# Sublayer outputs of a two-layer hybrid decoder: three projections from channels on the partitions to tokens on the partitions

## The chip, the cores and the metric

The kernel runs on one core of one Trainium2 chip. A core has TensorE (PE, matrix products into PSUM banks), VectorE (DVE), ScalarE (ACT), GpSimd (POOL) and SyncE (SP, which here issues DMAs). The metric is the device time of one execution, in microseconds; the median of several runs is compared.

## The reference

Batch 1, 512 tokens, model width 1024, two layers, all in float32. Layer 0 mixes tokens with an RG-LRU block, layer 1 with gated linear attention (GLA); each mixer is followed by a gated ConvFFN with 2816 hidden channels.

```python
c_act = silu(c)
for i in range(2):
    sh_m, sc_m, gt_m, sh_f, sc_f, gt_f = split(c_act @ ada_w[i] + ada_b[i], 6)
    h = rmsnorm(x, norm_g[i, 0]) * (1 + sc_m) + sh_m
    y = rglru_mixer(h) if i == 0 else gla_mixer(h)      # both end with  ... @ w_out  (1024 x 1024)
    x = x + gt_m * rmsnorm(y, norm_g[i, 1])
    h = rmsnorm(x, norm_g[i, 2]) * (1 + sc_f) + sh_f
    u = causal_dwconv3(h @ w_up); g, val = split(u, 2)
    y = (gelu(g) * val) @ w_down                        # 2816 x 1024
    x = x + gt_f * rmsnorm(y, norm_g[i, 3])
```

So there are four sublayers, each of which ends with a projection to y, a norm over the 1024 channels of y, a gated addition to the residual x and, but for the last, a norm over x and a scale and shift that make the next h. The change concerns the ends of the first three; the last one is already in the form that they get.

## The kernel before, in words

**Products.** Every float32 product is done as three matmuls on values that are split into a rounded high part and a low part: high x high, high x low, low x high (`mm3`, and the same three lines in `strassen` and `down_t`). A weight unit is 128 x 1024 floats (512 KB). SP loads it into a slot of the ring `raw` (3 slots), ScalarE casts the high part into a slot of the ring `w` (8 slots), and VectorE subtracts to get the low part. For the units that `BYLOAD` names, ScalarE writes the negated high part instead and a DMA from POOL's queue adds the unit from memory onto it. General tiles of 128 x 512 come from the ring `g` (43 slots), half ones from `gh`, products land in seven PSUM banks `mm`, small sums in an eighth, `nr`.

**A planner orders the work.** The program adds operations with a cost each to a list; `Sched.order` plays them on modelled engines and fixes the order of every engine's instructions and the slots. TensorE and SP take the ready operation that was added first; the others take the one with the longest modelled path behind it. On the chip each engine runs its instructions in that fixed order and waits on semaphores.

**Channels on the partitions.** x, h and the mixers' values lie with 128 channels on the partitions and tokens along the row. x fills `xbuf` in that form from the start. In `out_proj`, which ends the RG block, the first feed-forward layer and GLA, the weights are the stationary operand and the activations move. `FULL` (1, 2, 2) output tiles are computed over all 512 tokens; the others first over tokens 0 to 255, then 256 to 511, so that the first half's normalisation runs while TensorE works on the second half. A norm over channels is then a sum over partitions: ScalarE squares, VectorE adds the eight tiles, TensorE multiplies with a column of ones (`rstd_bcast`), POOL takes the power -0.5, TensorE broadcasts it. This is done once for y and once for the new x in each half: four times in each `out_proj`, twelve in all. The next projection begins in halves as well: `proj_halves` computes the first `NAH` = 7 units over one half of the tokens, then over the other.

**The feed-forward layers.** 22 pairs of hidden tiles (`up`) alternate with parts of the down projection. In layer 0 the hidden tiles are summed in `DOWN_GROUPS`: tiles 0-3 and 8-9 directly, 4-7 and 10-13 by Strassen's seven products (`strassen_cols`, moving width 256), 14-21 in `out_proj`. In layer 1 tiles 0-17 go through Strassen with the activations stationary and the weights moving, width 512 (`strassen`, groups of `SGROUPS`), and y has tokens on the partitions; tiles 18-21 follow directly in `down_t`. There x is turned by VectorE in two steps of 16 transposes of 32 x 32 blocks (`turn_x`), and `gate_rows` makes the gate as two rows over channels.

**adaLN.** The modulation columns are 1024-long products of c with rows of `ada_w`, 96 units of 512 KB, each one VectorE operation (`ada`). Sixteen are made at the start; 80 wait in `ada_queue` and are taken by `ada_some`: 24 (`ADA_A`) ahead of the RG output, 4 (`ADA_B`) behind it, 4 per pair (`ADA_F`) in layer 0's feed-forward until none is left. Their ring `araw` has two slots; the GLA's attention rows (`both` in `inter_mm`) and layer 1's hidden quarters use the same ring.

Of the kernel before, what the change touches and what calls it, by code (L numbers as in the profile page):

```python
# [8 lines left out]
F32 = mybir.dt.float32  # L9
# [18 lines left out]
DOWN_GROUPS = ((0, 4), (4, 8), (8, 10), (10, 14), (14, 22))  # L28

SGROUPS = ((0, 4), (4, 8), (8, 12), (12, 16), (16, 18))
SLAST = (18, 22)
SPARTS = (3,), (4, 2), (5, 6), (7, 1)
SFIRST = (1, 3)
# [11 lines left out]
def sunits(gi):  # L48

    a, b = SGROUPS[gi]  # L50
    if b - a == 4:
        return [((i, 0), (i, 1)) for part in SORDER for i in part]
    return [((3, 0), (4, 0)), ((2, 0), (5, 0)), ((6, 0), (7, 0)), ((1, 0),)]


def sfind(gi, i, j):

    for u in sunits(gi):
        if (i, j) in u:
            return ("st", gi, u), u.index((i, j))  # L60


def last_ffn():

    steps, done = [], 0
    for gi, (a, b) in enumerate(SGROUPS):
        for part in SORDER:
            while done < min(b + 1, KF):
                steps.append(("up", done))
                done += 1  # L70
            steps += [("st", gi, i) for i in part]
            b += 1
# [11 lines left out]
def unit_list():  # L84
# [12 lines left out]
    for m in range(KD):  # L97
        u.append((("rgo", m), "rg_w_out", [(k, m) for k in range(KD)]))
# [4 lines left out]

    def ffn(layer):
        if layer == 1:
            for what, *i in last_ffn():
                if what == "up":
                    pair(1, *i)
                    continue
                gi, n = i  # L110
                key, c = sfind(gi, n, 0)
                if c == 0:
                    a = SGROUPS[gi][0]
                    u.append((key, "dn1", [(a + 2 * j + SPROD[n_][0][0], 4 * SPROD[n_][0][1] + m)
                                           for n_, j in key[2] for m in range(4)]))
            for k in range(*SLAST):
                u.append((("dnt", k), "dn1", [(k, m) for m in range(KD)]))
            return
        done = 0
        for gi, (a, b) in enumerate(DOWN_GROUPS):  # L120
            if gi in SFIRST:
                while done < b + 1:
                    pair(layer, done)
                    done += 1
                for part in SPARTS:
                    for n in part:
# [1558 lines left out]
```

## Time and profile before

| | |
|---|---|
| runs, median (lowest to highest), 3 runs | 1146.86 us (1146.44 to 1147.57) |
| span of the profiled execution, first to last instruction | 1145.5 us |
| TensorE busy | 1130.3 us, 6219 instructions |
| VectorE busy | 973.1 us, 1734 instructions |
| ScalarE busy | 627.0 us, 993 instructions |
| GpSimd busy | 92.3 us, 115 instructions |
| read from memory | 203.0 MB, 179 GB/s over the span |

For the profiled execution nothing but its span is given; the runs' median lies 1.4 us above it. The stages in TensorE's timeline: the RG block's input projection from about 18 us, its output projection from about 132 to 182, the first feed-forward layer to about 542 (its `out_proj` from 508), GLA to about 800 (its output projection from about 745), then the second feed-forward layer. Line 552 is the one line that issues every matmul, 475, 489 and 500 VectorE's two-input, three-input and one-input operations, 525 and 532 ScalarE's, 480 POOL's power, 980 the transposes of x. Matmuls are pipelined, so the durations of single ones overlap, and a stretch's length over its count is the better price of one.

### The profile page before, as it was taken

What the parts mean: (1) busy time and instruction counts of PE and PEld (TensorE: products, weight loads), DVE (VectorE), ACT (ScalarE), POOL (GpSimd) and SP (SyncE); (2) the same over time, 40 slices, a digit from 0 to 9 for tenths busy, and PEclk for the clock granted to TensorE, in tenths of its full rate; (3) what the DMA queues carried; (4) which work ended last, traced back from release to release, by engine and by line L of the source; (5) the groups of instructions that cost most, each with busy time, mean ns of one, the idle gap of its engine ahead of it and who ended that gap; (6) DMA issues with size and microseconds to landing.
All of it is one profiled execution on the core that took longest, in us unless ns stands there. A gap on an engine that the chain in (4) does not pass through costs nothing.

```text
span 1145.5 us, 16668 instructions
## 1 busy us (share of the span) xinstructions
PE 1130.3 (99%) x6219; PEld 977.9 (85%) x6219; DVE 973.1 (85%) x1734; ACT 627.0 (55%) x993; POOL 92.3 (8%) x115
## 2 busy tenths in 40 slices
PE   8999999999999999999999999999999999999997
PEld 6876899988888888889997888899988888888886
DVE  7998999966888898788959989549788898999998
ACT  5499864655435444543559645445656545363443
POOL 1000000001000010000100100100010100101001
PEclk9999999999999999999999999999999999999999
DMA  9868663588777987964571703323366677878631
GB/s 368 294 207 282 205 237 112 165 249 239 201 193 222 262 257 202 288 206 146 141 228 44 189 14 112 125 59 86 81 154 177 162 178 193 201 186 203 147 111 74
DMA packets 57651, 206.19 MB, mean 180 GB/s; under 512 B 6401, under 2 KB 6913, under 8 KB 57570
## 3 DMA queue, kind: packets, MB, share of 16 engines
q1 hardware_dynamic: 46914, 166.59, 42.6%
q0 software_dynamic: 10656, 38.54, 19.3%
q8 instruction: 49, 0.80, 0.3%
q14 instruction: 32, 0.26, 0.1%
HBM read 203.00 MB, written 2.10 MB: 179 GB/s over the span
## 4 chain that ended last, share of the span: by engine, by line
PE 85%; DVE 6%; ACT 4%; issue 2%; DMA 1%; POOL 1%; DVEq 0%; SPq 0%; POOLq 0%; ACTq 0%
PE mm L552 83%; PE nr L552 2%; ACT g L525 2%; DVE gh L475 1%; DVE g L475 1%; ACT L525 1%; DVE const L475 1%; DVE gh L489 1%; DVE w L475 1%; POOL sm L480 1%; DMA araw<-in_adaT_dram 0%; DVE const L489 0%; ACT w L532 0%; DMA raw<-in_wall_dram 0%; DMA const<-in_xT_dram 0%
## 5 line engine op out<-in xcount | busy, mean ns | idle before, releaser
L552 PE MATMUL mm<-g,w 128*128 128x512 f32 (+1 forms) x4342 | 822.4, 349 | 0.1
L552 PEld LDWEIGHTS mm<-g,w 128*128 128x128 f32 x4342 | 702.7, 189 | 104.9 <-issue 1.4
L532 ACT CAST w<-raw 128x1024 fp32r<-128x1024 f32 x198 | 203.7, 1039 | 117.1 <-DMA raw<-in_wall_dram 84.7
L475 DVE TENSOR_TENSOR w<-raw,w 128x1024 fp32r<-128x1024 f32 x157 | 189.3, 1212 | 24.6 <-ACT w L532 24.3
L489 DVE SCALAR_TENSOR_TENSOR g<-mm,const,g 128x510 f32<-128x510 f32 (+2 forms) x199 | 147.1, 747 | 58.6 <-ACT g L525 48.1
L525 ACT ACTIVATE g<-mm,const 128x512 f32<-128x512 f32 (+1 forms) x144 | 101.2, 707 | 85.9 <-PE mm L552 83.0
L552 PE MATMUL mm<-w,g 128*128 128x512 f32 (+1 forms) x624 | 143.4, 386 | 0.0
L475 DVE TENSOR_TENSOR g<-g,g 128x256 f32<-128x256 f32 (+4 forms) x217 | 120.4, 580 | 20.0 <-ACT g L532 9.6
L552 PEld LDWEIGHTS mm<-w,g 128*128 128x128 f32 x624 | 115.1, 188 | 23.3
L475 DVE TENSOR_TENSOR g<-g,mm 128x512 f32<-128x512 f32 (+1 forms) x239 | 120.8, 560 | 6.7 <-PE mm L552 6.6
L525 ACT ACTIVATE g<-g 128x512 f32<-128x512 f32 (+1 forms) x139 | 71.1, 544 | 74.0 <-DVE g L489 51.0
L489 DVE SCALAR_TENSOR_TENSOR araw<-araw,const 128x1024 f32<-128x1024 f32 x72 | 87.2, 1221 | 11.2 <-DMA araw<-in_adaT_dram 10.9
L552 PE MATMUL mm<-g,g 128*128 128x256 f32 (+2 forms) x604 | 80.3, 288 | 0.0
L552 PEld LDWEIGHTS mm<-g,g 128*128 128x128 f32 x604 | 75.7, 191 | 1.4
L532 ACT CAST g<-g 128x512 fp32r<-128x512 f32 (+1 forms) x75 | 44.9, 604 | 55.0 <-DVE g L475 54.8
L563 POOL DMA_DIRECT2D w<-in_wall_dram x41 | 35.8, 873 | 467.9 <-ACT w L525 389.9
L525 ACT ACTIVATE w<-raw 128x1024 fp32r<-128x1024 f32 x41 | 43.3, 1056 | 23.9 <-DMA raw<-in_wall_dram 17.2
L475 DVE TENSOR_TENSOR gh<-gh,gh 128x256 f32<-128x256 f32 (+1 forms) x101 | 42.1, 423 | 14.6 <-ACT gh L525 12.3
L480 POOL TENSOR_TENSOR sm<-sm,const 128x2 f32<-128x2 f32 (+2 forms) x22 | 22.0, 999 | 344.8 <-DVE sm L500 274.3
L563 POOL DMA_DIRECT2D raw<-in_wall_dram x33 | 28.9, 875 | 153.7 <-DMA raw<-in_wall_dram 62.1
L525 ACT ACTIVATE g<-gh,const 128x256 fp32r<-128x256 f32 x48 | 22.3, 503 | 24.8 <-DVE gh L489 24.6
L525 ACT ACTIVATE gh<-const 128x256 f32<-128x256 f32 x48 | 18.8, 413 | 18.7 <-DVE const L475 18.6
(119 smaller groups left out, 737.9 us busy)
## 6 DMA issues: line engine op xcount, KB each, us to landing
raw<-in_wall_dram SPq DMA_DIRECT2D x211, 512.0 KB, 4.5
araw<-in_adaT_dram SPq DMA_DIRECT2D x72, 512.0 KB, 5.1
w<-in_wall_dram POOLq DMA_DIRECT2D x41, 512.0 KB, 7.6
raw<-in_wall_dram POOLq DMA_DIRECT2D x32, 512.0 KB, 6.9
w<-in_adaT_dram SPq DMA_DIRECT2D x24, 512.0 KB, 8.5
const<-in_xT_dram SPq DMA_DIRECT2D x4, 512.0 KB, 5.2
out_dram<-const SPq DMA_DIRECT2D x8, 256.0 KB, 2.0
araw<-in_masks_dram SPq DMA_DIRECT2D x1, 512.0 KB, 3.8
```

The source lines that it names most:

```text
L475: self.s.add(eng, dur, lambda: e.tensor_tensor(out.ap(), a.ap(), b.ap(), op=op), [a, b], [out])
L480: lambda: self.nc.gpsimd.tensor_tensor(out.ap(), a.ap(), b.ap(), op=ALU.pow), [a, b], [out])
L489: return self.nc.vector.scalar_tensor_tensor(out.ap(), a.ap(), f(sc), b.ap(), op0=op0, op1=op1, **kw)
L525: return self.nc.scalar.activation(out.ap(), a.ap(), func, **kw)
L532: self.s.add("act", (0.095 if self._sb(a) else 0.052) + out.n * 0.8325e-3, lambda: self.nc.scalar.copy(out.ap(), a.ap()), [a], [out], afte ...
L552: r.append(self.nc.tensor.matmul(g[0].ap(), g[1].ap(), g[2].ap(), start=g[3], stop=g[4], **kw))
L563: self.s.add("pool", 1.2, lambda: self.nc.gpsimd.dma_start(out.ap(), src, accum_op=ALU.add), [out], [out], xfer=nbytes / 180e3)
```

## The change

The three ends take the last layer's form. The output projection has the activations stationary and the weights moving at width 512, with y token-major: `down_pair` does token tiles 0 and 1, `down_t` tiles 2 and 3. A norm is then a sum along a row (ScalarE's square with an accumulated sum), and x is updated token-major; to that end x is loaded a second time, in that form, once the first h is made. The normalised x is turned back for h by TensorE, 32 transposes of 128 x 128 at each end, and ScalarE scales and shifts it out of PSUM. The gates become rows by `gate_rows` at each end. Both feed-forward layers use `strassen` at width 512 on 18 of the 22 hidden tiles, the mixers' outputs do not (their `SGROUPS` are empty). `NAH` goes from 7 to 4. `turn_x` goes. The adaLN columns are spread anew (26, 4, 1 per pair, and 2 per chunk in GLA), the `gr` units get their low part by DMA, the masks are loaded as bytes, and the planner's priorities see the ring `araw`.

```diff
-DOWN_GROUPS = ((0, 4), (4, 8), (8, 10), (10, 14), (14, 22))
-SGROUPS = ((0, 4), (4, 8), (8, 12), (12, 16), (16, 18))
-SLAST = (18, 22)
+SGROUPS = {"rg": (), "gl": (),
+           "f0": ((0, 4), (4, 8), (8, 12), (12, 16), (16, 18)),
+           "f1": ((0, 4), (4, 8), (8, 12), (12, 16), (16, 18))}
+SLAST = {"rg": (0, 8), "gl": (0, 8), "f0": (18, 22), "f1": (18, 22)}
...
+        for cls in RINGS:
+            ring = sorted((b for b in self.bufs if b.cls == cls and b.ops), key=lambda b: b.ops[0])
+            for b, later in zip(ring, ring[self.slots[cls]:]):
+                for i in b.ops:
+                    if i < later.ops[0]:
+                        extra[i].append(later.ops[0])
...
+    def turn(self, out, a, ident):
+        self.s.add("pe", 0.112, lambda: self.nc.tensor.transpose(out.ap(), a.ap(), ident.ap()), [a, ident], [out])
...
-BYLOAD = lambda what, *i: what in ('rgg', 'gv') or ...
+BYLOAD = lambda what, *i: what in ('rgg', 'gv', 'gr') or ...
-FULL = (1, 2, 2)
-NAH = 7
+NAH = 4
+LASTK = 2
-XT_AT = 8, 12
-ADA_A, ADA_B, ADA_F = 24, 4, 4
+ADA_A, ADA_B, ADA_F, ADA_G = 26, 4, 1, 2
...
-    def out_proj(src, wkey, klist, gate, nexth, yacc=None):
...
-    def proj_halves(keys, h_):
+    def proj_halves(keys, h_, steps):
         ws = [unit(*k) for k in keys]
         pss = [mmtile() for _ in keys]
         for sl in HALVES:
+            next(steps)
...
+    def down_pair(sub, hid, ts):
+        a, b = SLAST[sub]
+        out = [[mmtile() for _ in range(2)] for _ in ts]
+        for k0, k1 in ((a, b - LASTK), (b - LASTK, b)):
+            for t, pss in zip(ts, out):
+                tok = slice(t * P, (t + 1) * P)
+                for k in range(k0, k1):
+                    w = unit("dnt", sub, k)
+                    hi, lo = (v[tok] for v in hid[k])
+                    for f, ps in enumerate(pss):
+                        c = f * S
+                        e.mms([(ps[:], hi, w[c:c + S], k == a, False), (ps[:], lo, w[c:c + S], False, False),
+                               (ps[:], hi, w[D + c:D + c + S], False, k == b - 1)])
+        return [[ps[:] for ps in pss] for pss in out]
...
+    def sublayer_out(sub, src, y, gate, nexth):
+        layer, gpart = gate
+        hl, hlayer, hpart = nexth
+        rows = gate_rows(layer, gpart, (len(s.ops) - 1,))
+        xn = {}
+        def residual(t, pss):
+            ss, s2 = s.buf("sm", F32, 4), s.buf("sm", F32, 4)
+            ys = []
+            for f, ps in enumerate(pss):
+                sq = gt()
+                if y[2 * t + f] is None:
+                    yv = gt()[:]
+                    e.act(sq[:], ps, AF.Square, accum=ss[f:f + 1])
+                    e.tt(yv, ps, rows[f][:], ALU.mult)
+                else:
+                    yv = y[2 * t + f][:]
+                    e.tt(yv, yv, ps, ALU.add)
+                    e.act(sq[:], yv, AF.Square, accum=ss[f:f + 1])
+                    e.tt(yv, yv, rows[f][:], ALU.mult)
+                ys.append(yv)
+            rp = rstd_col(ss, 2)
+            for f, yv in enumerate(ys):
+                xr = xrows(t, f * S, (f + 1) * S)
+                e.stt(xr, yv, rp, xr, ALU.mult, ALU.add)
+                sq = gt()
+                e.act(sq[:], xr, AF.Square, accum=s2[f:f + 1])
+            rp2 = rstd_col(s2, 2)
+            for f in range(2):
+                xn[t, f] = gt()
+                e.act(xn[t, f][:], xrows(t, f * S, (f + 1) * S), AF.Copy, scale=rp2)
+        def turned(half):
+            sl = HALVES[half]
+            for f in range(2):
+                banks = [mmtile(), mmtile()]
+                for t in (2 * half, 2 * half + 1):
+                    for k in range(4):
+                        c = k % 2 * 256 + t % 2 * P
+                        e.turn(banks[k // 2][c:c + P], xn[t, f][k * P:(k + 1) * P], ident[:])
+                for k in range(4 * f, 4 * f + 4):
+                    hv = gtn(256)
+                    e.act(hv, banks[k % 4 // 2][k % 2 * 256:(k % 2 + 1) * 256], AF.Identity,
+                          scale=mcol(hlayer, hpart + 1, k), bias=mcol(hlayer, hpart, k))
+                    e.ts(hl[k][0][sl], hv, 1.0, None, ALU.mult)
+                    e.tt(hl[k][1][sl], hv, hl[k][0][sl].f32(), ALU.subtract)
+        for t, pss in enumerate(down_pair(sub, src, (0, 1))):
+            residual(t, pss)
+        turned(0)
+        def rest():
+            for t in (2, 3):
+                residual(t, down_t(sub, src, t))
+            yield
+            turned(1)
+            yield
+        return rest()
...
-        def strassen_cols(gi, i):
...
-        def down(gi):
...
+        for what, *i in ffn_steps(sub):
+            if what == "up":
+                up(*i)
+            else:
+                first = len(s.ops)
+                strassen(sub, *i, hid, y)
+                s.steps += range(first, len(s.ops))
+        if layer == 1:
+            last_down(hid, y, grow)
+        else:
+            return sublayer_out(sub, hid, y, (0, 5), nexth)
...
+    for t in range(NT):
+        e.load(xbuf[t * D:(t + 1) * D], x_d[t], P * D * 4)
...
-    out_proj(ysp, lambda m: ("rgo", m), list(range(KD)), (0, 2), (h, 0, 3))
+    steps = mixer_out("rg", ysp, (0, 2), (h, 0, 3))
     h2 = new_h()
     ada_some(ADA_B)
-    ffn(0, h, (h2, 1, 0), ADA_F)
+    steps = ffn(0, h, steps, (h2, 1, 0), ADA_F)
...
-    mtmp = s.buf("araw", F32, D)
-    e.load(mtmp[:], masks_d, P * D * 4, late)
-    e.dve(0.6, lambda: nc.vector.tensor_copy(masks[:].ap(), mtmp[:].ap()), [mtmp[:]], [masks[:]])
+    e.load(masks[:], masks_d, P * D, late)
...
+        ada_some(ADA_G)
...
-    out_proj(osp, lambda m: ("go", m), list(range(KD)), (1, 2), (h, 1, 3))
-    ffn(1, h, None, 0)
+    steps = mixer_out("gl", osp, (1, 2), (h, 1, 3))
+    ada_some(len(ada_queue))
+    ffn(1, h, steps, None, 0)
```

371 lines of the change are left out of this document (135 added, 236 removed).

## The prediction

> **What bounds the kernel now.** First the busy shares on the page, then whom TensorE waited for, then stretches in which it runs one kind of matmul (columns: stretch, its length, busy time and records of each engine, clock, DMA share, GB/s).
>
> ```profile
> span 1145.5 us, 16668 instructions
> ## 1 busy us (share of the span) xinstructions
> PE 1130.3 (99%) x6219; PEld 977.9 (85%) x6219; DVE 973.1 (85%) x1734; ACT 627.0 (55%) x993; POOL 92.3 (8%) x115
> ```
> ```profile
> PE nr L552 <- DVE gh L475: 3.0, 2, 2.7
> PE mm L552 <- DMA araw<-in_c_dram: 2.3, 1, 2.3
> PE nr L552 <- POOL sm L480: 0.6, 2, 0.3
> PE mm L552 <- DVE g L475: 0.6, 2, 0.4
> ```
> ```profile
> 205.00:221.00 16.00, 16.00 (x136) 16.00 (x135) 14.18 (x22) 8.01 (x12) 0.00 (x0) 1.00 0.56 198
> 460.00:505.00 45.00, 45.00 (x200) 37.24 (x200) 34.91 (x48) 24.37 (x32) 1.72 (x2) 1.00 0.79 245
> 1030.00:1120.00 90.00, 90.00 (x399) 74.50 (x398) 86.58 (x126) 38.29 (x49) 6.04 (x7) 1.00 0.56 146
> 1125.00:1146.00 21.00, 12.28 (x66) 10.48 (x64) 15.51 (x33) 6.82 (x17) 3.21 (x4) 0.88 0.26 101
> ```
>
> A busy TensorE can be a stretched one, so I take its rate. The first stretch holds only 128x256 matmuls: 136 records less about two counted at the edges, 0.120 us each. The second holds only 128x512 with weights stationary, the third only 128x512 with activations stationary (the last feed-forward layer, already token-major): less two at the edges, 0.227 us each in both. So two halves cost 0.240 us where one full matmul costs 0.227, and it does not matter which operand is stationary. The waits add up to 6.5 us, of which the two longest (2.7 and 2.3) belong to the start; the last row's 8.7 us without a matmul are the tail. Start and tail are left as they are. In between the time is the sum of TensorE's instructions, and a change is worth what it takes off that sum, less the waits it opens.
>
> **TensorE's sum.** Out go, at width 256: the RG output projection's 7 tiles x 2 halves x 24 = 336; the 6 halved tiles of the first feed-forward layer's last group, 288, and of the GLA output, 288; that layer's two Strassen groups, 2 x 168 = 336; and in each of three following projections three units that are no longer halved (7 halved ones become 4), 3 x 144 = 432. 1680 x 0.120 = 201.6 us. At width 512: out go 24 + 48 + 48 full-width products and the direct groups' 96 + 48, together 264; in come 192 (RG) + 192 (GLA), in the feed-forward layer four groups of 84, one of 42 and 96 at the end = 474, then 216 for the units no longer halved and 12 for three new pairs of gate rows, together 1086. Net 822 x 0.227 = +186.6 us.
>
> Each of the twelve normalisations in the old output code also puts two groups of four small fp32 records on TensorE, a column sum and a broadcast. The timeline of TensorE, with starts in the first column:
>
> ```profile
> 187.26 0.60 PE L552 MATMUL nr<-const,sm 128*128 128x128 f32 x4
> 187.62 3.48 PE L552 MATMUL mm<-g,w 128*128 128x256 f32 x27
> 190.94 5.92 PE L552 MATMUL mm<-g,g 128*128 128x256 f32 x48
> 196.69 0.50 PE L552 MATMUL nr<-const,gh 128*128 128x1 f32 x4
> 197.06 2.02 PE L552 MATMUL mm<-g,g 128*128 128x256 f32 x15
> 198.92 0.60 PE L552 MATMUL nr<-const,sm 128*128 128x128 f32 x4
> 199.28 0.96 PE L552 MATMUL mm<-g,g 128*128 128x256 f32 x6
> ```
>
> From start to next start such a group takes 0.36 to 0.37 us, so 24 x 0.37 = 8.9 us go. In come 96 transposes of 128x128 fp32. The trace has none. A record with 128 fp32 weight columns takes 0.09 us in these rows whether 1 or 128 columns move, so loading the weights sets it, and a transpose loads as many: 0.09 is the lower end (8.6 us). The upper end is that a transpose is two such records, as these products are (four records for two products): 0.18 (17.3 us). I take one record, as an identity needs no second part, but 0.105 of it, between 0.09 and the 0.120 of the 128x256: 10.1 us. The Trainium skill, "TensorE: Matmul & The Clock Gate", section Terms, says that the transpose mode of load and matmul is four times faster for FP32; by it the streaming stays below the load and the sum is as taken; no run here shows it yet.
>
> Sum: -201.6 + 186.6 - 8.9 + 10.1 = -13.8 us.
>
> **Waits at the three sublayer ends.** Before:
>
> ```profile
> 131.00:177.00 46.00, 45.59 (x350) 43.84 (x349) 44.39 (x86) 26.47 (x55) 1.59 (x2) 1.00 0.58 191
> 553.00:600.00 47.00, 46.65 (x335) 43.83 (x334) 35.74 (x73) 25.76 (x43) 6.41 (x11) 1.00 0.71 206
> ```
>
> 0.41 and 0.35 us idle at the first two: these 0.8 us go. After, the critical chain starts when token tile 3's matmuls end. Its steps are the kinds of these rows (groups by shape; the number ahead of the second bar is the mean of one in ns):
>
> ```profile
> L525 ACT ACTIVATE g<-mm 128x512 f32<-128x512 f32 x28 | 16.5, 595 | 15.2 <-PE mm L552 15.1
> ...
> L525 ACT ACTIVATE g<-mm,const 128x256 f32<-128x256 f32 x26 | 12.3, 473 | 0.0
> ...
> L525 ACT ACTIVATE g<-g,const 128x512 fp32r<-128x512 f32 x7 | 5.1, 724 | 2.2 <-DVE g L489 2.2
> ...
> L525 ACT ACTIVATION_READ_ACCUMULATOR g<-g 128x1 f32 x7 | 1.3, 186 | 0.0
> ```
> ```profile
> L480 POOL TENSOR_TENSOR sm<-sm,const 128x1 f32<-128x1 f32 x4 | 2.9, 724 | 56.6 <-DVE sm L489 56.6
> ```
> ```profile
> L475 DVE TENSOR_TENSOR w<-raw,w 128x1024 fp32r<-128x1024 f32 x155 | 188.4, 1221 | 24.6 <-ACT w L532 24.3
> L489 DVE SCALAR_TENSOR_TENSOR araw<-araw,const 128x1024 f32<-128x1024 f32 x72 | 87.2, 1221 | 11.2 <-DMA araw<-in_adaT_dram 10.9
> L475 DVE TENSOR_TENSOR g<-g,mm 128x512 f32<-128x512 f32 x129 | 81.4, 682 | 2.6 <-PE mm L552 2.6
> ...
> L475 DVE TENSOR_TENSOR g<-g,mm 128x256 f32<-128x256 f32 x110 | 39.4, 417 | 4.1 <-PE mm L552 4.0
> ...
> L489 DVE SCALAR_TENSOR_TENSOR const<-g,sm,const 128x512 f32<-128x512 f32 x6 | 4.3, 744 | 0.0
> ```
>
> Two squares with sums 2 x 0.78, mean 0.3 (an estimate), power 0.72, two residual updates 1.49, the last square 0.78, mean 0.3, power 0.72, two scaled copies 1.45, transposes 0.4, first scale-and-shift 0.47, rounding 0.3 (below the 0.42 of a 256-column operation): 8.5 us. The old chain gives the hand-overs: from 187.26 to 196.69 it takes 9.4 us for a broadcast (0.36), sixteen VectorE operations of 0.42, a square and an addition (0.84), so about 1.5 us for some six changes of engine, 0.25 each with what else stood in the queues. Eleven make 2.8: 11.3 us, and 1.4 more at the feed-forward end (two additions of 0.68). The cover is half of the next projection, 96 x 0.120 = 11.5 us (GLA: 8.6, and some 1.9 of the narrow z unit), and 16 transposes, 1.7: 13.2 us, and 12.2 for GLA. Nearly even: 0 to 2 us per end, I take 2 us for the three. The bounds are 0 and the first rival. Late next come weights: the eight output units fill the w ring until tile 3 has passed, and the next projection's first units are cast (1.22 us each on VectorE) behind them.
>
> **Other engines and queues.**
>
> ```profile
> 55.00:70.00 15.00, 15.00 (x65) 12.01 (x64) 13.67 (x31) 12.15 (x17) 1.75 (x2) 1.00 1.04 338
> 223.00:508.00 285.00, 285.00 (x1419) 242.85 (x1418) 228.87 (x386) 141.16 (x183) 23.30 (x27) 1.00 0.81 230
> 588.00:745.00 157.00, 156.21 (x874) 133.87 (x873) 133.38 (x262) 96.61 (x186) 10.91 (x12) 1.00 0.35 102
> ```
>
> *First feed-forward layer.* VectorE gains 31 us of additions to y (120 of 512 columns at 81.4/129 = 0.63 for 108 of 256 at 0.36 and 10 of 512), 17 us of quarter sums (five more pairs of tiles, each 3.3 us: a sum and a third low part 1.36, four operations of 256, 0.3 of split products) and 10 us for eight more weight units; it loses 30 adaLN columns at 1.3 (22 run there instead of 52), 39 us, and about 12 us of operations of 256 columns at its end. Net +7 on 229 of 285 us: hidden. The second layer shows the same form running dense, VectorE at 86.58 of 90 us; the 32 transposes of x by VectorE leave that layer, where they were hidden. *GLA.* 28 columns come, +34 to 37 us, through the two-slot ring that also holds attention rows; eight low parts move to accumulating DMAs, -10 us. 133 becomes some 158 of 157 us, with 11 us free in the 47 ahead (35.74 busy). The cover is gone there: bounds 0 and 8 us of wait, I take 1.5. ScalarE's eight negations of about 1 us on 97 of 157 are hidden. POOL issues 21 more accumulating DMAs, at 8% busy; a power queued behind one waits for its issue. SP issues eight more units, four 512 KB loads of x, a smaller mask. The x loads can start when the first h is made, after 50 us, and meet full queues (share 1.04): 2 MB at 338 GB/s delay the gate weights by up to 6 us. Bounds 0 and 6; I take 0.5, as adaLN columns give way first.
>
> Sum: -13.8 - 0.8 + 2 + 1.5 + 0.5 = -10.6 on a span of 1145.5: 1134.9. The runs' median, 1146.86, is 1.4 above that span: 1136 us.
>
> **Rivals.** *The boundary wait (slower).* If each of the chain's eleven steps meets half a running operation of 1.2 us, it becomes 11.3 + 6.6 = 17.9 us against 13.2: 4.7 us of wait at each end. A cold start may follow:
>
> ```profile
> 18.40:21.00 2.60, 2.60 (x14) 2.60 (x13) 2.60 (x6) 1.17 (x3) 0.00 (x0) 1.00 1.04 398
> 21.00:23.40 2.40, 2.40 (x21) 2.40 (x21) 2.40 (x4) 0.95 (x2) 0.00 (x0) 1.00 1.02 406
> ```
>
> Both hold 128x256 matmuls, first at 0.21 us, then at 0.12 (the clock column says 1.00 twice). Three microseconds of that behind each wait cost 1.3 more: 6.0 x 3, less the 2 taken, 1152 us. The same page of the Trainium skill, Part 1, halves the clock after an idle window of about 3.4 us; the rows agree on the factor, 1.75, only roughly and do not show the trigger. The rival decides from 5 us lost per end (10.9 + 2.3 us more than taken). For it: VectorE at 44.39 of 46 us at the first end. Against: the old chain there was covered to 0.4 us. Chance 0.13.
> *GLA becomes VectorE's*: 8 us lost, 1142.5. For it: 158 of 157. Against: columns can run ahead of the stage. 0.12.
> *Transposes take two records*: 17.3 for 10.1, 1143; with 0.21 each, 1146. For it: every fp32 product here has two. 0.11.
> *My forecast*, 1128 (no new waits, 0.09 per transpose) to 1141 (waits doubled): 0.64.
>
> A measurement of this kernel tells about 0.2% (2.3 us) from no change. Faster: 0.64, and most of the two cases near 1143, 0.76; same 0.10; slower 0.14. The range, 1127 to 1146, leaves out the boundary wait and a little below.
>
> **What would show it.** 5361 TensorE records (858 fewer matmuls, 96 fewer small ones, 96 transposes of one record each); about 1116 us busy; transposes 0.1 us apart; under 1 us idle at each sublayer end; VectorE near 100% in GLA and PE still dense. I am wrong if TensorE is named as waiting for ACT or DVE at transposes or at the first h of a half, if matmuls run at 0.21 us behind such a wait, or if transposes stand 0.2 us apart.

## The result: 0.5% slower, TensorE's work gone as forecast and its waits come instead

The changed kernel takes 1153.47 us (median of 4, 1152.12 to 1153.86); beside it on the same chip the kernel before took 1146.73. The ratio is 1.0053, 95% interval 1.0039 to 1.0067. The forecast was 1136 us, with 1127 to 1146 as range: it was wrong by 17 us and in its sign. The profiled execution of the changed kernel took 1152.12 us, with a span of 1150.3. One execution of e4 below, 1246.79 us at a granted clock of 0.851, was in a slower state of the chip and is left out, and since it was the profiled one, e5 runs e4's kernel again.

The page of the changed kernel, its busy shares and the chain that ended last:

```profile
span 1150.3 us, 15016 instructions
...
PE 1118.4 (97%) x5361; PEld 928.3 (81%) x5361; DVE 961.9 (84%) x1671; ACT 669.5 (58%) x1051; POOL 124.3 (11%) x148
...
PE 65%; ACT 12%; DVE 10%; DMA 8%; issue 2%; POOL 1%; SPq 0%; DVEq 0%; ACTq 0%; POOLq 0%
```

TensorE has 5361 records, the forecast number, and 11.9 us less busy time (1130.3 to 1118.4). But the span less its busy time grew from 15.2 to 31.9 us: -11.9 + 16.7 = +4.8 us of span. ScalarE, VectorE and DMA now carry 30% of the chain that ended last. Whom TensorE waited for:

```profile
PE mm L547 <- DVE g L470: 3.9, 3, 2.4
PE mm L554 <- ACT gh L520: 3.0, 3, 2.1
PE nr L547 <- DVE g L470: 2.8, 1, 2.8
PE mm L554 <- ACT g L520: 2.8, 5, 1.3
PE nr L547 <- DVE gh L470: 2.7, 1, 2.7
PE mm L547 <- DMA araw<-in_c_dram: 2.5, 1, 2.5
PE nr L547 <- POOL sm L475: 1.9, 1, 1.9
PE mm L547 <- ACT g L520: 1.7, 3, 1.3
```

The old list had two waits of over 0.4 us, both at the start (here 2.7 and 2.5). The new ones lie in every stage but the last. By stretches (RG output and first boundary; first feed-forward layer; its end; GLA and its end), before:

```profile
115.00:223.00 108.00, 107.59 (x806) 103.08 (x805) 101.65 (x194) 68.39 (x126) 5.32 (x6) 1.00 0.55 180
...
508.00:600.00 92.00, 91.59 (x705) 88.26 (x704) 73.97 (x164) 43.78 (x82) 9.53 (x14) 1.00 0.58 177
600.00:830.00 230.00, 228.91 (x1503) 207.37 (x1502) 186.03 (x378) 137.35 (x268) 16.08 (x17) 1.00 0.32 90
```

and after:

```profile
115.00:223.00 108.00, 102.67 (x552) 87.26 (x551) 93.70 (x176) 82.73 (x144) 10.16 (x12) 1.00 0.57 171
223.00:508.00 285.00, 282.29 (x1243) 232.77 (x1242) 247.78 (x384) 146.05 (x188) 32.81 (x38) 1.00 0.86 231
508.00:600.00 92.00, 89.23 (x487) 75.85 (x486) 75.62 (x155) 71.34 (x134) 11.65 (x17) 1.00 0.52 158
600.00:830.00 230.00, 223.97 (x1275) 193.10 (x1274) 186.15 (x380) 139.02 (x262) 31.22 (x30) 1.00 0.55 158
```

Idle TensorE: 5.3, 2.7, 2.8 and 6.0 us, 16.8 in all, where 1.9 us stood. VectorE's busy time tells nothing of it: in the last stretch it is the same to 0.1 us. What grew there is DMA, from 90 to 158 GB/s.

The chain of waits, followed back from a wait, names what was late. The longest behind 115 us, in GLA, ends at 649 us. First the transfer in the chain, then three rows of the timeline of all engines, each with the idle time ahead of it and what ended that:

```profile
632.29 12.75 DMA raw<-in_wall_dram
```
```profile
645.14 1.06 ACT L520 ACTIVATE w<-raw 128x1024 fp32r<-128x1024 f32 x1 [5.15 <-DMA raw<-in_wall_dram]
...
648.77 1.37 DVE L470 TENSOR_TENSOR g<-g,g 128x512 f32<-128x512 f32 x3 [3.01 <-ACT g L520]
...
649.52 0.72 PE L547 MATMUL nr<-const,g 128*128 128x1 f32 x5 [2.80 <-DVE g L470]
```

A weight unit took 12.75 us from issue to landing (median of these transfers on the page: 4.7). ScalarE stood for 5.15 us at the operation that needs it, and everything behind it in ScalarE's queue, the operands of VectorE's and so of TensorE's next work too, waited. The same with 5.30 us ahead of the transposes at 199 us:

```profile
191.77 5.30 DMA raw<-in_wall_dram
197.07 0.02 issue
197.09 1.04 ACT w L527
198.14 0.93 ACT gh L520 x2
```

The scale-and-shift of the turned x (ACT gh) was ready to go and stood behind the cast of a weight. So the transposes' 2.06 us, put down to "ACT gh", are a late transfer's: at 5.30 us it is not a long one, but it was issued only at 191.77 us. At the RG output the chain of the same kernel (127 to 141 us) is ScalarE's alone:

```profile
by line: ACT g L520 36.2%; ACT w L527 27.7%; ACT L520 27.5%; ACT g L527 13.8%; issue 2.8%
```

"ACT L520" without a tile is a load of a function table.

### The profile page after: what moved, and what is told of

It reads as the page before. It is cut to its first block, busy times and chain, and to the rows that moved or that the text cites. A ratio compares the mean times of both kernels' runs of the same rounds, so it can differ in the third digit from the quotient of the medians.

```text
span 1150.3 us, 15016 instructions
## 1 busy us (share of the span) xinstructions
PE 1118.4 (97%) x5361; PEld 928.3 (81%) x5361; DVE 961.9 (84%) x1671; ACT 669.5 (58%) x1051; POOL 124.3 (11%) x148
## 4 chain that ended last, share of the span: by engine, by line
PE 65%; ACT 12%; DVE 10%; DMA 8%; issue 2%; POOL 1%; SPq 0%; DVEq 0%; ACTq 0%; POOLq 0%
PE mm L547 64%; DMA raw<-in_wall_dram 6%; ACT g L520 6%; DVE g L470 3%; ACT w L527 2%; ACT L520 2%; DVE w L470 2%; DVE g L484 1%; DMA araw<-in_adaT_dram 1%; DVE w L484 1%; ACT w L520 1%; DVE araw L484 1%; POOL sm L475 1%; PE nr L547 1%; ACT g L527 1%
## 5 line engine op out<-in xcount | busy, mean ns | idle before, releaser
L547 PE MATMUL mm<-g,w 128*128 128x512 f32 (+2 forms) x2758 | 614.3, 380 | 0.1
L547 PEld LDWEIGHTS mm<-g,w 128*128 128x128 f32 (+1 forms) x2758 | 501.4, 188 | 99.3 <-issue 1.4
L547 PE MATMUL mm<-w,g 128*128 128x512 f32 (+1 forms) x1428 | 332.8, 389 | 4.0 <-DVE g L470 3.8
L547 PEld LDWEIGHTS mm<-w,g 128*128 128x128 f32 x1428 | 264.9, 188 | 59.6 <-DVE g L470 5.0
L484 DVE SCALAR_TENSOR_TENSOR g<-mm,const,g 128x510 f32<-128x510 f32 (+3 forms) x199 | 146.6, 747 | 55.0 <-ACT g L520 46.0
L470 DVE TENSOR_TENSOR g<-g,g 128x256 f32<-128x256 f32 (+3 forms) x264 | 142.5, 568 | 34.0 <-ACT g L520 23.8
L470 DVE TENSOR_TENSOR g<-g,mm 128x512 f32<-128x512 f32 (+1 forms) x241 | 153.3, 681 | 15.1 <-PE mm L547 13.0
L520 ACT ACTIVATE g<-mm,const 128x512 f32<-128x512 f32 x115 | 86.8, 761 | 83.3 <-PE mm L547 81.1
L520 ACT ACTIVATE g<-g 128x512 f32<-128x512 f32 (+1 forms) x147 | 76.1, 549 | 82.7 <-DVE g L484 60.5
L547 PE MATMUL mm<-g,g 128*128 128x256 f32 (+3 forms) x508 | 78.4, 309 | 0.2 <-DVE g L470 0.2
L547 PEld LDWEIGHTS mm<-g,g 128*128 128x128 f32 (+1 forms) x508 | 70.4, 191 | 5.7 <-DVE g L470 0.6
L520 ACT ACTIVATE w<-raw 128x1024 fp32r<-128x1024 f32 x49 | 51.8, 1058 | 39.7 <-DMA raw<-in_wall_dram 38.3
L475 POOL TENSOR_TENSOR sm<-sm,const 128x1 f32<-128x1 f32 (+2 forms) x34 | 35.9, 1057 | 283.4 <-DVE sm L484 191.7
L520 ACT ACTIVATE g<-mm 128x512 f32<-128x512 f32 x44 | 25.9, 595 | 20.7 <-PE mm L547 11.0
L520 ACT ACT_TABLE_LOAD x24 | 30.8, 1283 | 1.1 <-PEq L1669 0.7
## 6 DMA issues: line engine op xcount, KB each, us to landing
const<-in_x_dram SPq DMA_DIRECT2D x4, 512.0 KB, 10.7
```

What stands on the lines that cost most here:

```text
L470: self.s.add(eng, dur, lambda: e.tensor_tensor(out.ap(), a.ap(), b.ap(), op=op), [a, b], [out])
L475: lambda: self.nc.gpsimd.tensor_tensor(out.ap(), a.ap(), b.ap(), op=ALU.pow), [a, b], [out])
L484: return self.nc.vector.scalar_tensor_tensor(out.ap(), a.ap(), f(sc), b.ap(), op0=op0, op1=op1, **kw)
L520: return self.nc.scalar.activation(out.ap(), a.ap(), func, **kw)
L547: r.append(self.nc.tensor.matmul(g[0].ap(), g[1].ap(), g[2].ap(), start=g[3], stop=g[4], **kw))
```

## The experiments

Seventeen experiments with sixteen kernels. Ratios are to the kernel before on the same chip, with 95% intervals. "Idle" is 1010 us less TensorE's busy time between 115 and 1125 us of the profiled execution: 1.9 before, 16.8 after. Single waits are read off TensorE's timeline, as the time between two starts beyond the usual one for that kind.

**e1_cols_f0.** The adaLN columns go back from GLA to the first feed-forward layer.

```
-ADA_A, ADA_B, ADA_F, ADA_G = 26, 4, 1, 2
+ADA_A, ADA_B, ADA_F, ADA_G = 26, 4, 4, 0
```

> The adaLN columns that the change moved into GLA go back into the first feed-forward layer (4 per pair, none in GLA); all else as in the changed kernel. In its trace TensorE waits 3.0 us at 646 and 2.0 us at 654, with the DMA queues at a share of 1.04 from 630 to 655 and ScalarE idle from 640 to 645. Theory A, the 28 columns overload GLA: these 5 us go, TensorE's idle time between 600 and 700 falls below 1 us, and at most 2 us come back in the first feed-forward layer, whose VectorE gets 37 us more: about 1149 to 1151. Rival B, the eight units whose low part now comes by an accumulating DMA hold ScalarE and the queues: the 5 us stay, and the time is 1153 or, with VectorE fuller ahead of the first feed-forward end, 1155 to 1160.

1152.78 us, 1.0047 [1.0030, 1.0063], idle 16.7. The waits of GLA did not go but stand later, at 677 to 699 us (8.3 us), and two of their chains are 39 and 68% an adaLN row's transfer. But the edit did not do what it was meant to. It moves the columns in the program's list; the planner put them back. All operations on the ring `araw` in GLA, in the changed kernel and here (VectorE's time is the third after the stretch's length):

```profile
588.00:745.00 157.00, 5.84 (x18) 3.02 (x18) 29.20 (x50) 2.51 (x7) 1.00 0.62 178
```
```profile
588.00:745.00 157.00, 8.13 (x24) 4.27 (x24) 32.58 (x56) 2.89 (x8) 0.99 0.63 183
```

VectorE's whole time in the first feed-forward layer rose by 1.2 us (247.78 to 248.93), not by the 37 that 28 columns would take. Whether the columns in the stage make the waits is not tested here; e16 comes nearest to it.

**e2_gr_dve.** The low parts of the eight gr units by VectorE again, not by accumulating DMAs (`'gr'` taken out of BYLOAD).

> The eight gr units get their low part from VectorE again, as before the change, instead of a negation by ScalarE and an accumulating DMA; the columns stay in GLA. Theory B, the accumulating DMAs make the GLA waits: the 5 us between 644 and 656 go, 1148 to 1150. Theory A, the columns do: the waits stay, and VectorE has 10 us more in a stage where it is at 21 to 24 of 25 us: 1153 to 1158.

1152.64 us (1148.85 to 1162.06), 1.0054 [1.0033, 1.0075], idle 16.0. One wait of 2.1 us stays at 649 us, another of 1.7 us comes at 760 us. No gain.

**e3_nah6.** `NAH = 6` for 4: six units of a projection run by halves, so half of the next projection covers the boundary for longer.

> NAH 6 instead of 4: six units of the next projection run in halves, so the cover of the second half's chain grows by 48 matmuls of width 256, 5.8 us. Theory C, the waits on the transposes (2.1 at 199, 1.3 at 539, 1.3 at 555 to 558, 1.0 at 779 and 802) come from a cover that is too short: the second-half ones (2.1, 1.3, 0.5) go, 2 us of width-256 price are added: 1151 to 1153. Rival D, the chain is held up by what is queued on ScalarE and VectorE, which grows with the units to be cast: the waits stay or move, 1155 to 1160.

1152.12 us, 1.0045 [1.0028, 1.0061], idle 15.6. The transposes' waits become one of 1.27 us at each end, and others open (4.5 us from 467 to 483 us, 1.7 at 758 us). More cover at the boundaries alone gains nothing.

**e4_gate_late.** The gate rows' matmuls are issued behind the output products of the first two token tiles; before, TensorE's order put them first.

```
-        rows = gate_rows(layer, gpart, (len(s.ops) - 1,))
+        late = (len(s.ops) - 1,)
+        pairs = down_pair(sub, src, (0, 1))
+        rows = gate_rows(layer, gpart, late)
...
-        for t, pss in enumerate(down_pair(sub, src, (0, 1))):
+        for t, pss in enumerate(pairs):
```

> The four matmuls that make the gate rows at a sublayer's end are put behind the products of token tiles 0 and 1 in TensorE's list instead of ahead of them; nothing else is changed, though the planned order shifts. Theory E, the matmuls stand in TensorE's queue before ScalarE and VectorE have made their operands: the waits at 143 to 145 (about 1 us) and at 505 to 507 (1.5 us) go, 1150.5 to 1152. Rival: the waits only move to the products behind, since the splits that these need are late as well (the 2.4 us at 138 stay): 1153 within 1.

1147.80 us (median of nine), 1.0008 [0.9998, 1.0018]: 5 us of the loss is won back by order alone.

**e5_gate_late2.** e4's kernel again, for its trace.

> The kernel of e4 (the gate rows' matmuls issued behind the output products of a half, not ahead of them) once more, for its trace. Theory 1 (the waits opened by the order of TensorE's queue at the ends, gate rows first, are a third of what was lost): 1147 to 1149 us, no wait of over 0.5 us in front of the first RG output product (2.55 us at 138.5 us in the changed kernel) or of the gate rows of the feed-forward layer (1.49 us at 505.1 us); what is left are the transposes (about 2 us at 199 us, 1.5 at 555 us, 0.7 at 778 us) and the 1.5 us at 482 us. Rival (the waits are a fixed lateness of VectorE and ScalarE and only change their place): the list of TensorE's waits has the same 2 to 3 us elsewhere, at the first products of the next half, and the sum of waits behind 115 us stays at 18 to 20 us.

1149.92 us, 1.0024 [1.0013, 1.0035], idle 11.7. The gate rows no longer hold TensorE up at 505 us; the RG output still does (1.55 and 0.69 us at 137 to 139 us), and 2.6 us at 464 to 468 us and 3.2 us at 583 us are new. So part of each theory holds: order is worth 3 to 5 us, and other waits take places of their own. The longest, at 583 us, in stretches and by its chain:

```profile
575.00:583.00 8.00, 5.21 (x23) 3.97 (x22) 4.12 (x7) 4.10 (x6) 0.86 (x1) 0.99 1.06 283
583.00:588.00 5.00, 4.62 (x11) 3.65 (x12) 3.05 (x5) 2.97 (x4) 0.00 (x0) 0.50 1.03 356
588.00:600.00 12.00, 12.00 (x51) 9.85 (x50) 8.06 (x16) 11.87 (x21) 0.00 (x0) 0.93 0.11 45
```
```profile
566.48 12.89 DMA araw<-in_adaT_dram
579.38 0.02 issue
579.40 0.04 DVE araw L484
```

An adaLN row took 12.89 us while the DMA engines were full (1.06, 1.03), VectorE stood at it, and after 3.2 us of wait TensorE ran at a granted clock of 0.50: 13 matmuls at 0.43 us for 0.227 and one before them at 0.59, 3.0 us more. Straight after, DMA is nearly idle (0.11). The transfers bunch.

**e7_one_norm.** e4's kernel with `rp2 = rp` for the second norm's square, mean and power: a chain shorter by an estimated 2.2 us.

> e4's kernel without the second of the two norms of each token tile (the power of the first is used twice), so the output is not the reference's; the chain between a tile's last product and its transposes is shorter by a square with its sum, a mean and a power, about 2.2 us. Theory 2 (the chain's length makes the waits of the transposes at the sublayer ends): the waits in front of transposes, 2.06 us at 197 us, 1.4 to 1.8 us at 537 to 557 us and 1.3 us at 778 to 801 us, fall to under 0.3 us each, and the time to 1143 to 1145 us. Rival (they come from the work queued ahead on ScalarE and VectorE, whatever the chain's length): at least half of each wait stays and the time is 1147 to 1149 us.

1144.85 us (1141.44 to 1150.00), 0.9983 [0.9966, 1.0000], idle 10.8. At two of the three ends one wait of 0.62 us is left, at the third 1.56 us, and a GLA wait of 2.85 us with 3.2 us lost in slow matmuls stands at 641 us, in a profiled execution of 1148.86 us. The chain's length counts for 3 to 5 us by the ratios to e4 and e5, with the work that it saves ScalarE.

**e8_f0_16.** e4's kernel with the first feed-forward layer's Strassen groups up to tile 16 and six tiles taken directly.

```
-           "f0": ((0, 4), (4, 8), (8, 12), (12, 16), (16, 18)),
+           "f0": ((0, 4), (4, 8), (8, 12), (12, 16)),
...
-SLAST = {"rg": (0, 8), "gl": (0, 8), "f0": (18, 22), "f1": (18, 22)}
+SLAST = {"rg": (0, 8), "gl": (0, 8), "f0": (16, 22), "f1": (18, 22)}
```

> e4's kernel with the first feed-forward layer's Strassen groups on 16 of the 22 tiles instead of 18: six more matmuls of 128x512 (by 0.227 us +1.4 us on TensorE), some 15 us of additions to y and 3 us of quarter sums less on VectorE, and a direct group of six tiles at the end. Theory 3 (the wait of 1.54 us at 482 us and what follows it at the layer's end come from VectorE's backlog of additions to y): these waits go, the net is 0 to -1 us, 1146 to 1148 us. Rival (the backlog there has slack and the waits come from banks that are freed late by hand-overs): the 1.54 us stay and the time is 1149 to 1150 us.

1139.43 us (1138.17 to 1139.88), 0.9935 [0.9920, 0.9949]: faster than both kernels, and by far more than either side expected. Its chain and its stretches:

```profile
PE 91%; DVE 3%; ACT 3%; DMA 2%; issue 1%; POOL 0%; DVEq 0%; SPq 0%; ACTq 0%; POOLq 0%
```
```profile
115.00:223.00 108.00, 105.06 (x557) 89.38 (x556) 94.13 (x181) 81.56 (x140) 9.57 (x12) 0.98 0.61 190
223.00:508.00 285.00, 285.00 (x1260) 236.04 (x1259) 246.39 (x378) 153.87 (x202) 30.32 (x35) 1.00 0.85 237
508.00:600.00 92.00, 91.54 (x505) 79.34 (x504) 65.37 (x137) 67.78 (x125) 11.60 (x19) 1.00 0.47 133
600.00:830.00 230.00, 228.16 (x1296) 197.75 (x1295) 189.29 (x385) 136.52 (x259) 28.06 (x31) 1.00 0.54 161
```

Idle 2.9, 0, 0.5 and 1.8 us, 5.2 in all: of single waits over 1 us only the RG output's is left (1.9 us at 138 us, 0.7 behind it). VectorE has 246.39 us in the feed-forward layer's 285, as in the changed kernel (247.78), and TensorE does not wait: the load of the stage as a whole was not it.

**e9_after_16.** The same edit on the changed kernel itself, gate rows left ahead.

> The changed kernel itself with one edit: the first feed-forward layer's Strassen groups end at tile 16, not 18, and six tiles are taken directly. Theory 3 (the backlog of VectorE in that layer is the largest part of what was lost): the wait of 1.54 us at 482 us, the 1.8 us of the transposes at 555 us and the 5 us in the GLA stage (646 to 656 us) go, +1.4 us of matmuls come, 1142 to 1146 us. Rival (the gain seen with the gate rows moved needs that move; alone the gate rows' matmuls still hold up TensorE): 1149 to 1152 us.

1146.36 us (1143.28 to 1150.27, 10 runs), 0.9996 [0.9984, 1.0007], idle 10.5. 7 us are won without the move of the gate rows; the waits at 482 us and of the transposes at 555 us go (0.62 us left), but 0.9 and 2.1 us in GLA with 1.6 us of slow matmuls stay. By the ratios this edit is worth 6.5 us and e4's 3 to 5; together, in e8, they are worth 13.5, which looks like more than the sum but, with 95% intervals of 1 to 2 us to either side of each ratio, is not shown to be.

**e10_narrow_y.** e5's kernel; the fifth Strassen group's 24 additions to y move 32 of 512 columns, in the same order.

> The kernel with the gate rows behind the output products and all 18 Strassen tiles (1150 us), in which the 24 additions to y of the fifth group (tiles 16 and 17 of the first feed-forward layer) take 32 of 512 columns, so that the output is not the reference's; weights, matmuls and the order of every queue stay. VectorE has some 12 to 13 us less to do between 455 and 490 us. Theory 3 (VectorE's load in that stretch): the waits of 4.5 us between 464 and 482 us go and the time is 1139 to 1144 us. Rival (the six-tile direct group at the layer's end, longer by a third, or its eight weight units less, is what helped): 1148 to 1151 us.

1148.18 us (1143.67 to 1151.86), 1.0003 [0.9988, 1.0018], idle 11.3. TensorE's waits between 455 and 485 us:

```profile
PE mm L547 <- DVE g L470: 2.0, 1, 2.0
PE mm L547 <- ACT g L527: 0.3, 1, 0.3
```

The wait of 2.0 us at 468 us stays; those of 1.7 us at 478 to 481 us go. Between 474 and 487 us the traces with 18 tiles and whole additions have 1.5 to 2.8 us of waits (0.5 in e14, whose order differs), the two with narrow additions (e10, e17) none. VectorE's additions cost that much; the theory of their backlog as the main cause falls.

**e11_lastk4.** e8's kernel, `LASTK = 4` for 2: the last four k (tiles of 128 input channels) of the output products stand behind the first four.

> e8's kernel (16 Strassen tiles in the first feed-forward layer, gate rows behind the output products) with the last four k of the first two token tiles' output products put behind their first ones, where the last two were (LASTK 4 for 2); number and kind of instructions stay. Theory 1 (TensorE waits at the RG output for the last ysp splits, 1.9 + 0.7 + 0.4 us and five slow matmuls at 137 to 143 us): these 4 us shrink to under 2 us, 1136 to 1139 us. Rival (the chain through ScalarE and VectorE there is late by a fixed amount, and the next k waits as long): 1139 to 1141 us.

1139.83 us, 0.9939 [0.9920, 0.9958], idle 7.0. The waits at 137 to 143 us go and two of 1.2 and 2.1 us come ahead of the output (117 and 134 us). ScalarE is late there, whatever TensorE's order.

**e12_no_acc.** e5's kernel; the fifth group's three accumulating weight transfers carry 32 columns.

> The kernel with 18 Strassen tiles and the gate rows behind the output products (1148 to 1150 us), in which the three accumulating weight transfers of the fifth group (raw += second quarter, 512 KB twice and 256 KB) carry 32 columns of 1024, so that three Strassen weight sums are left out and the output is not the reference's; the order of every queue and the number of instructions and transfers stay. Theory 4 (weight transfers that land late, with ScalarE's cast, VectorE's low part and the next split waiting in order behind them): the chain that ends in the waits at 464 to 468 us loses 2 to 4 us, these waits fall from 3 us with five slow matmuls to under 1 us, and the time is 1142 to 1146 us. Rival (order and hand-overs only): the waits of 464 to 483 us stay, 1147 to 1150 us.

1150.74 us (1146.08 to 1152.52), 1.0027 [1.0008, 1.0045], idle 11.0. The wait at 464 to 468 us is 0.4 us in its trace, but e16, which leaves these transfers alone, has none either; and the time did not fall. As a cause these three transfers are not shown.

**e13_tb5.** e8's kernel with a dearer change of table in the planner (`TABLE_BIAS` 5 for 3), which orders ScalarE's queue anew.

> The kernel with 16 Strassen tiles and the gate rows behind the output products (1139.4 us), with the weight that the planner gives a change of ScalarE's function table raised from 3 to 5 us: only the order of ScalarE's queue and what follows from it changes, with three table loads less, all between 100 and 145 us (1.28 us each). Theory 5 (ScalarE, kept busy by table loads ahead of the RG output, makes TensorE wait there for the last gated products: 1.87 + 0.7 + 0.36 us and five slow matmuls at 137 to 143 us): these 4 us fall under 2 us, 1136 to 1138.5 us. Rival (ScalarE is late there by its casts of weights): the waits stay, 1138.5 to 1141 us.

1139.19 us (1137.10 to 1143.25), 0.9933 [0.9911, 0.9955], idle 6.6. The RG waits fall only from 2.6 to 2.1 us. The profiled execution was the slowest (1143.25): a GLA wait of 1.5 us, and after it half the clock.

```profile
638.70:640.30 1.60, 0.25 (x2) 0.00 (x0) 0.73 (x2) 1.48 (x5) 0.00 (x0) 1.00 1.07 284
640.40:647.20 6.80, 6.80 (x21) 5.58 (x22) 6.24 (x16) 2.41 (x7) 1.95 (x1) 0.54 0.98 312
```

**e14_plan_late.** The changed kernel; its planner takes accumulating transfers to land 1 us later (`dma_free + 4.5` for 3.5).

> The changed kernel itself with one edit in the planner: an accumulating transfer is taken to land 1 us later than before when the queues are written out. Work, transfers and matmuls stay as they are; only the order on the queues changes, so that casts stand further behind their transfers. Theory 4b (the order puts work in front of late transfers, and in-order queues pass the lateness on): the waits at 482, 505 and 646 to 656 us fall by half or more, 1144 to 1149 us. Rival (the transfers themselves are late whatever the order, since the layer's load and accumulate chains have no slack): 1151 to 1156 us.

1154.04 us, 1.0052 [1.0037, 1.0068], idle 15.1. The waits at 482 to 505 us shrink to 1.2, and 3.7 us at 142 us and 4.5 us at 581 us come. A more careful order of this kind does not help.

**e15_both.** e13's kernel with e14's edit.

> e13's kernel with e14's edit too: 16 Strassen tiles, gate rows behind the output products, dearer table changes, and accumulating transfers planned 1 us later. If both theories hold, 1134 to 1138 us and under 5 us of TensorE's waits behind 115 us; if order alone does nothing more, 1138 to 1141 us; if the planner's pessimism costs TensorE time, 1141 to 1146 us.

1139.93 us, 0.9937 [0.9922, 0.9951], idle 5.6. No more than e8.

**e16_gla_rows.** e5's kernel; each adaLN row that GLA loads is half as long and multiplied twice.

> The kernel with 18 Strassen tiles and the gate rows behind the output products (1148 to 1150 us), in which each adaLN row that the GLA stage loads brings 512 of its 1024 columns and is multiplied and summed in two operations of 512, so that some columns of the last layer's modulation are left out; VectorE's time stays within 3 us, some 7 MB of transfers go. Theory 6 (the rows moved into the GLA stage make its transfers bunch, and VectorE, waiting in order for a row, stops TensorE): the wait of 3.0 to 3.6 us at 577 to 580 us with its slow matmuls (2 us) goes and none of over 1 us appears between 570 and 760 us: 1143 to 1147 us. Rival (the weights alone bunch): a wait of 2 us or more stays between 570 and 660 us, 1148 to 1151 us.

1143.95 us, 0.9977 [0.9958, 0.9997], idle 8.8: 4 to 5 us less by the ratios, in the range expected. Nothing of over 1 us stands between 585 and 790 us. But the wait at 577 to 580 us is shorter (2.3 us), not gone, as the rival said: its row still took 11.58 us. And the trace does not account for the time: against e5's, idle time and slow matmuls around 580 us are 2.3 us less, and another 1.7 us of idle time went in the first feed-forward layer, whose rows this edit leaves alone.

**e17_all.** e16 with the leave-outs of e10 and e12.

> The same with the two other leave-outs as well: the fifth Strassen group's additions to y on 32 columns and its three accumulating transfers with 32 columns. All 18 tiles' matmuls stay. If the named causes (late accumulating transfers 3.7 us, additions to y 1.7 us, GLA rows 5 us) are the whole of what ending the groups at tile 16 saves, 1138 to 1142 us and TensorE's waits behind 115 us are under 9 us, as with 16 tiles. If the order at the layer's end (a longer direct group) is what helps, 1144 to 1148 us.

1142.45 us, 0.9952 [0.9936, 0.9969], idle 8.0. Waits between 455 and 485 us, then from 545 to 660 us:

```profile
PE mm L547 <- DVE g L470: 0.2, 1, 0.2
```
```profile
PE mm L547 <- DVE g L470: 1.9, 1, 1.9
PE mm L554 <- ACT g L520: 0.9, 2, 0.7
PE mm L554 <- ACT gh L520: 0.5, 1, 0.5
```

The layer is dense with all 18 tiles. The time lies between the two ranges and decides for neither "the named causes are the whole" nor the order at the layer's end. What e8 has in hand beside it is what these rows hold: 1.4 us of transposes, and 1.9 us with 1.6 us of slow matmuls at 577 us.

**e18_no_sqrt.** e8's kernel; the RG recurrence's square root is a copy (`AF.Copy` for `AF.Sqrt`, no table).

> The kernel with 16 Strassen tiles and the gate rows behind the output products (1139.4 us), in which the square root in the RG recurrence is a copy, so that the output is not the reference's; an operation on ScalarE stays in its place, but the function tables of the square root are never loaded, some four to six loads of 1.28 us less ahead of the RG output. Theory 5 (table loads make ScalarE late there): the waits at 137 to 143 us (2.9 us and five slow matmuls, 1 us) fall under 1 us, 1135 to 1137.5 us. Rival (casts and other work): they stay, 1138 to 1140 us.

1141.02 us, 0.9940 [0.9925, 0.9955], idle 6.2. Table loads between 100 and 145 us, in the kernel before, the changed one, e8 and this one:

```profile
L525 ACT ACT_TABLE_LOAD x4 | 5.1, 1283 | 0.1
```
```profile
L520 ACT ACT_TABLE_LOAD x8 | 10.3, 1283 | 0.1
```
```profile
L520 ACT ACT_TABLE_LOAD x10 | 12.8, 1283 | 0.2
```
```profile
L520 ACT ACT_TABLE_LOAD x5 | 6.4, 1283 | 0.1
```

TensorE's waits from 115 to 210 us:

```profile
PE mm L554 <- ACT gh L520: 2.1, 1, 2.1
PE mm L554 <- ACT g L520: 1.8, 1, 1.8
PE mm L547 <- DVE w L470: 0.5, 1, 0.5
```

The RG output's wait falls from 2.6 us to 0.5 with five loads fewer. ScalarE's order changed with them, and e13 and e15, with seven loads, still wait 2.1 and 2.6 us there; so the loads have a part in this wait, but they alone are not shown to make it. And 3.9 us come at the transposes 35 to 60 us later, so nothing is won.

## Why the prediction was wrong

*TensorE's sum* was right. Forecast -13.8 us; busy time fell by 11.9, with stretched and half-rate matmuls in it. e8, with six matmuls more (+1.4), has 1117.9 us busy, so 1116.5 without them, and 1116 was forecast. Transposes are single records: 96 of them, ten in 1.25 us, the last of 0.27, so (1.25 - 0.27) / 9 = 0.109 us apart where 0.105 was taken. The rival of two records falls.

```profile
195.79 1.25 PE L554 MATMUL mm<-const,g 128*128 128x128 f32 x10
199.11 0.66 PE L554 MATMUL mm<-const,g 128*128 128x128 f32 x4 [2.06 <-ACT gh L520]
```

*The waits* were wrong: -0.8 + 2 + 1.5 + 0.5 = +3.2 us forecast, 14.9 measured from 115 to 1125 us (16.8 less 1.9). Three terms failed.

1. *The three sublayer ends, +2.* The chain of eleven steps was compared with its cover as if it ran alone. Measured were 2.6 us (167 to 199), 3.3 us (537 to 558) and 1.3 us (778 to 801), 7.2 in all. The rival with half a running operation in front of each step had the right sign and, at 4.7 us per end, the wrong mechanism and price: at 199 us the step did not meet a running operation but one that waited for a transfer, in a queue that keeps its order.
2. *The entries of the output products and the gate rows, no term at all.* "Late next come weights" was as far as it went. The RG output lost 2.55 us and 0.85 at its gate rows, the gate rows at 505 us 1.5. At the RG output the diagonals of the gate rows and twice as many table loads (8 for 4) came to ScalarE just there, which was busy for 23.99 of the 25 us from 125 to 150 us; the RG row quoted for VectorE (44.39 of 46) was the wrong engine's. At 505 us ScalarE loaded no table. It waited 2.72 us for a weight before it made the diagonals, and the chain there is 71% weight transfers, the last of them

```profile
496.04 7.47 DMA raw<-in_wall_dram
```

At both places the gate rows' matmuls stood ahead of output products; put behind them, in e5's trace, they cost nothing at 505 us and still 0.65 us at the RG output.

3. *First feed-forward layer and GLA, "hidden" and +1.5.* Both were judged by VectorE's sums. In the layer VectorE was forecast at 236 of 285 us; it had 247.78, and 246.39 in e8 where nothing waits. In GLA it was forecast at 158 of 157; it had 134.44, 1 us more than before, and on the ring `araw` 29.20 us where it had 10.05, not the 34 to 37 more that were forecast. The waits were 1.5 us at 484 us in the layer, and 3.0, 2.0 and 0.5 us in GLA, at 649, 656 and 724 us. What had grown stands in the last columns:

```profile
588.00:745.00 157.00, 151.92 (x841) 129.54 (x840) 134.44 (x273) 94.22 (x180) 21.07 (x19) 1.00 0.62 178
```

102 GB/s became 178, 16.0 to 27.9 MB in that stretch, and the transfers bunch to a share of 1.0 and single ones of 12.8 us. The wait at 649 us is such a transfer's; that the added bytes make the bunching was not tested by itself. Of this the prediction priced only the x loads, at 0.5 us; and those cost nothing seen (TensorE is busy for all of 50 to 75 us, though they took 10.7 us to land).

Counted from start to start, the waits named in 1 to 3 add up to 19 us, somewhat more than the idle time. One of them, at 656 us, is POOL's: GLA's power of 128x4 took 4.63 us (TensorE 1.9 us idle behind it); the four of 128x4 took 2605 ns on average, for 1339 before. Why is not shown: no run changed it alone. The power of 128x1 that the chain of the ends has, taken at 0.72 us, took 0.85 on average.

What is shown: order (e4) is worth 3 to 5 us and the 16 tiles (e9) 6 to 7, and together they give most of the forecast gain: 1139.4 us with 1.4 us of added matmuls, where the same steps forecast 1137.4. What stays open is which part of the 16 tiles does it. Narrow additions alone (1.7 us in the trace), light accumulations alone (nothing in the time) and half rows in GLA (4 to 5 us) make 1142.5 together and not 1139.4; the six tiles taken directly at the layer's end were not tested without the rest of the edit; and single waits of 2 to 3 us come and go between kernels that do not differ there. Executions of one kernel differ as well: 1143.67 to 1151.86 us for e10 and 1143.28 to 1150.27 for e9, ten each, and 1138.17 to 1139.88 for the four of e8, though e11 and e13, built on e8, reach 1145.04 and 1143.25. That long transfers vary from execution to execution is argued from that; it was not measured by itself.

## What to carry to other kernels

When TensorE is 99% busy, taking instructions from it buys their time (here 11.9 us of busy time for 13.8 forecast), provided that every engine and queue that feeds it keeps its slack; so for each stage write down the bytes per us and the in-order queue of ScalarE as well as VectorE's sum. Follow a wait's chain back past the engine it is put down to: "waits for ACT" or "for DVE" was a weight transfer three times (199, 507 and 649 us), and once ScalarE's own queue with its table loads (141 us). And count in the trace what an edit moved: in e1 the planner undid it. Before giving up a change that lost, look for its least valuable part: dropping 1.4 us worth of TensorE's saving (tiles 16 and 17) won 6 to 7 us.

## What the runs showed of the hardware

- Half the granted clock came after short waits: 3.2 us idle in e5 and then 13 matmuls of width 512 at 0.43 us (clock 0.50, 3.0 us lost), but also 1.4 us idle in e13 and then 13 of them (0.54, 3.2 us lost), while after the changed kernel's 2.4 us at 141 us they went on at 0.23 us. The Trainium skill, "TensorE: Matmul & The Clock Gate", Part 1, ties the half rate to an idle window of about 3.4 us that runs freely; the rows agree on the factor and show it after waits shorter than that.
- A load of a function table took 1283 ns on average in each of the four kernels under e18, and the next operation started 0.01 us behind it (changed kernel, load at 126.24 us, next operation at 127.53).
- With the DMA engines at a share of 1.05 (630 to 645 us of the changed kernel) a transfer of 512 KB took 12.75 us, beside a median of 4.7.
